# The last output projection of a two-layer decoder as Strassen's product of 7 for 8 (Winograd's form)

## The chip, the cores and the metric

One core of a Trainium2 chip. The time is device microseconds (us) of one execution. The engines are TensorE (PE: matrix products, and PEld, the loading of the stationary operand), VectorE (DVE), ScalarE (ACT), GpSimd (POOL) and SyncE (SP), whose queue issues nearly all transfers.

## The reference

Two layers on 1024 tokens of width 1024, in float32, each adding a normalized branch to its input, x <- x + RMSNorm_post(mixer(RMSNorm_pre(x))). Layer 0 is sliding-window attention. Layer 1 is a gated linear recurrence with 8 heads of 128:

```
proj = h @ w_in                      # q, f, i, z: 1024 columns each
o = chunked_gated_recurrence(silu(q), k(f), i, log_f(f))
o = o * rsqrt(mean(o * o) + eps) * gnorm_w        # per head
o = o.reshape(B, T, 1024) * silu(z)               # the gate
return o @ w_out                     # 1024 x 1024: the product that is changed
```

Call A the gated o (tokens x features) and B the matrix w_out (features x columns).

## The kernel before

**Precision.** Every matrix product of float32 operands is made of three TensorE products. Each operand is split in two parts of TensorE's float32 format: the high part is a rounded copy (ScalarE or GpSimd), the low part is what is left (VectorE). `product` (L219) issues high by high, high by low and low by high into the same PSUM bank.

**Weights.** All weight matrices lie in DRAM as blocks of 128x512 in the order of their use; 116 to 131 are w_out (first eight: columns 0 to 511, eight feature blocks; then columns 512 to 1023). `fetch` loads them on SP's queue into four raw buffers (`wraw`), `advance` splits them (`whi` on ScalarE L179, `wlo` on VectorE L180) into ten pairs of buffers, as soon as `used` has counted that the block which held the pair has served its last product. Before, each block of w_out serves eight units.

**Units.** `proj_nat(first, t)` (L243) computes 128 tokens (tile t) by 512 columns: eight feature blocks by three products, 24 instructions on TensorE into one bank. The activations are the stationary operand, in `act[k, half]` (feature block k, 512 tokens; `acth` and `actl`), the weights the moving one. PSUM has two banks for each of four tags (`mm`, `t`, `s`, `o`); a bank is written again only after it was emptied.

**Layer 1** (`mixer1`). First the value projections `i_unit(0, t)` of the first four heads (L876 empties them), beginning while the last rows of layer 0 are still normalized and transposed (L280, L204, L210); then, head by head, the query and gate projections `qf_unit` (L897 multiplies a query by its sigmoid, straight from the bank) with the recurrences `rec(h)` between them, which use the buffers `yn` and `S`; then the gate units `z_unit` (sigmoid on ScalarE, product on VectorE L1079, multiplication into `vo` on GpSimd L1080). `gated(half, ks)` transposes the gated o back on TensorE (L1071) and splits it from PSUM into `act` (L204, L210).

**The output projection** (`output1`): for both column halves c and eight token tiles t, one unit, then the sum of squares (ScalarE L1117), the product with the norm weight (VectorE L1118), and, when c is 1, the inverse root (GpSimd L258, L260), two VectorE instructions that scale a row and add x (L1131), and two stores. The last unit is cut in two halves of 256 columns. The second half of the last transposes comes behind the first unit.

**Order.** Each engine works through its own queue in the order in which a scheduler placed the program's instructions at build time; an instruction that waits holds up all behind it on that engine.

## Time and profile before

| what | us |
|---|---|
| three runs, median (lowest to highest) | 900.06 (899.93 to 900.25) |
| the profiled execution | 900.95 |
| its span | 899.1 |
| TensorE busy, share of the span | 878.8, 98% |
| VectorE busy | 556.3, 62% |
| ScalarE busy | 401.5, 45% |
| GpSimd busy | 326.1, 36% |

Times in the views are counted from the span's start. A row of a timeline gives start, length (of a run of like instructions, with their count), engine, line, operation, output and inputs, shapes, and in brackets how long the engine was idle before it and what released it. Matrix products overlap: the step from one start to the next is what one costs, not its length. A run's length with a count covers all of them. In the windows, columns are the engines' busy time in that stretch with the number of instructions, the granted TensorE clock, the share of the DMA engines, and GB/s.

### The profile page before, as it was taken

The numbers are of one execution on the slowest core, as the hardware profiler recorded it, in microseconds if no ns is written. First come the engines' busy times: TensorE is split into PE (matmuls) and PEld (weight loads), VectorE is DVE, ScalarE is ACT, GpSimd is POOL, SyncE is SP. The second block draws the span as 40 slices with busy tenths as digits, with TensorE's granted clock in tenths as the row PEclk, the third lists the DMA queues.
The fourth block names the chain that finished last, engine by engine and source line by source line (L and its number), as shares of the span: only waits on it lengthen the run. The fifth ranks groups of instructions, "written<-read, shape, count | busy, mean of one in ns | idle before, by whom it ended". The sixth has DMA issues, their size and how long they took to land.

```text
span 899.1 us, 14318 instructions
## 1 busy us (share of the span) xinstructions
PE 878.8 (98%) x5286; PEld 732.2 (81%) x5286; DVE 556.3 (62%) x900; ACT 401.5 (45%) x1048; POOL 326.1 (36%) x492
## 2 busy tenths in 40 slices
PE   6999999999999999999999999999999999999996
PEld 5887888888888888778888888888888788888885
DVE  7898887677898346852187873336877824262343
ACT  5635777767788233543223432333334224151211
POOL 4542644655676203320243532014434433220011
PEclk9999999999999999999999999999999999999998
DMA  9766455322132125422211010211111003041053
GB/s 339 266 201 184 136 169 142 92 71 82 48 92 82 47 95 175 154 106 72 70 48 36 17 43 1 83 49 34 37 36 48 1 1 94 1 135 53 24 187 121
DMA packets 55639, 82.61 MB, mean 92 GB/s; under 512 B 5128, under 2 KB 25224, under 8 KB 55560
## 3 DMA queue, kind: packets, MB, share of 16 engines
q1 hardware_dynamic: 55280, 81.54, 28.7%
q8 instruction: 43, 0.70, 0.3%
q14 instruction: 36, 0.29, 0.1%
q10 hardware_dynamic: 280, 0.07, 0.0%
HBM read 62.88 MB, written 16.88 MB: 89 GB/s over the span
## 4 chain that ended last, share of the span: by engine, by line
PE 78%; DVE 8%; issue 4%; DMA 4%; POOL 3%; ACT 1%; SPq 0%; DVEq 0%; POOLq 0%; ACTq 0%
PE psmm L222 48%; PE psmm L88 16%; PE pss L88 3%; PE pso L88 2%; DMA wraw<-in_w 2%; POOL rstd L260 2%; PE psk L1044 1%; PE pst L88 1%; PE pso L1057 1%; PE pso L1059 1%; POOL ms L258 1%; DMA xt<-in_xt 1%; PE pst L1038 1%; PE pst L1071 1%; DVE actl L88 1%
## 5 line engine op out<-in xcount | busy, mean ns | idle before, releaser
L222 PE MATMUL psmm<-whi,acth 128*128 128x512 f32 (+1 forms) x488 | 190.4, 391 | 1.1 <-DVE y L823 1.1
L222 PE MATMUL psmm<-whi,actl 128*128 128x512 f32 (+1 forms) x488 | 188.7, 388 | 0.0
L222 PE MATMUL psmm<-wlo,acth 128*128 128x512 f32 (+1 forms) x488 | 188.7, 387 | 0.0
L180 DVE TENSOR_TENSOR wlo<-wraw,whi 128x512 fp32r<-128x512 f32 x120 | 87.6, 740 | 94.1 <-ACT whi L179 88.6
L88 PE MATMUL psmm<-acth,whi 128*128 128x512 f32 x272 | 110.7, 407 | 1.7 <-ACT whi L88 1.7
L179 ACT ACTIVATE whi<-wraw 128x512 fp32r<-128x512 f32 x112 | 70.1, 630 | 87.9 <-PE psmm L222 66.9
L222 PEld LDWEIGHTS psmm<-whi,acth 128*128 128x128 f32 x488 | 91.7, 188 | 20.2 <-DVE y L823 1.8
L88 PE MATMUL psmm<-actl,whi 128*128 128x512 f32 x272 | 107.6, 396 | 0.2 <-DVE actl L88 0.2
L88 PE MATMUL psmm<-acth,wlo 128*128 128x512 f32 x272 | 107.7, 396 | 0.0
L222 PEld LDWEIGHTS psmm<-whi,actl 128*128 128x128 f32 x488 | 91.7, 188 | 18.4
L222 PEld LDWEIGHTS psmm<-wlo,acth 128*128 128x128 f32 x488 | 91.7, 188 | 17.9
L222 PE MATMUL psmm<-acth,whi 128*128 128x512 f32 x256 | 101.1, 395 | 0.2 <-DVE qf L897 0.2
L222 PE MATMUL psmm<-acth,wlo 128*128 128x512 f32 x256 | 100.4, 392 | 0.0
L222 PE MATMUL psmm<-actl,whi 128*128 128x512 f32 x256 | 100.2, 392 | 0.0
L708 ACT ACTIVATE sm<-sm,st 128x129 f32<-128x129 f32 x128 | 49.9, 392 | 26.6 <-DVE st L706 26.5
L88 PEld LDWEIGHTS psmm<-acth,wlo 128*128 128x128 f32 x272 | 51.7, 190 | 11.7 <-DVE wlo L88 0.2
L905 POOL TENSOR_SCALAR gate<-gate,lbt 128x512 f32<-128x512 f32 x16 | 17.8, 1111 | 118.9 <-ACT gate L903 108.4
L88 PEld LDWEIGHTS psmm<-acth,whi 128*128 128x128 f32 x272 | 52.0, 191 | 10.5 <-ACT whi L88 2.0
L88 PEld LDWEIGHTS psmm<-actl,whi 128*128 128x128 f32 x272 | 51.9, 191 | 8.7 <-DVE actl L88 0.7
L222 PEld LDWEIGHTS psmm<-acth,whi 128*128 128x128 f32 x256 | 48.1, 188 | 10.7 <-DVE qf L897 0.9
L222 PEld LDWEIGHTS psmm<-acth,wlo 128*128 128x128 f32 x256 | 48.1, 188 | 10.0
L222 PEld LDWEIGHTS psmm<-actl,whi 128*128 128x128 f32 x256 | 48.1, 188 | 9.5
(268 smaller groups left out, 1624.6 us busy)
## 6 DMA issues: line engine op xcount, KB each, us to landing
wraw<-in_w SPq DMA_DIRECT2D x132, 256.0 KB
QS<-qd SPq DMA_DIRECT2D x16, 512.0 KB
xr<-in_x SPq DMA_DIRECT2D x8, 512.0 KB
x1d<-xn SPq DMA_DIRECT2D x8, 512.0 KB
xr<-x1d SPq DMA_DIRECT2D x8, 512.0 KB
out_dram<-xn SPq DMA_DIRECT2D x16, 256.0 KB
o<-in_xt SPq DMA_DIRECT2D x8, 256.0 KB
xt<-in_x SPq DMA_DIRECT2D x4, 512.0 KB
```

What stands on the lines that cost most here:

```text
L88: return (lambda *a, **k: self.tc.keep_in_program_order(f(*a, **k))) if self.on else f
L179: nc.scalar.activation(hi, raw, AF.Copy)
L180: W["split_ins"][i] = v.tensor_tensor(lo, raw, hi.bitcast(F32), op=ALU.subtract)
L222: W["mm"] = pe.matmul(ps, a, b, start=(k == 0 and i == 0), stop=(k == NK - 1 and i == 2))
L258: keep(g.tensor_scalar(m, ms, eps, 1.0, op0=ALU.add, op1=ALU.mult))
L260: W["rstd"] = keep(g.tensor_tensor(r, m, nhalf[:, :width], op=ALU.pow))
L708: W["exp"] = nc.scalar.activation(sm[:, h, :], sm[:, h, :], AF.Exp, bias=nm[:, h:h + 1], scale=-1.0, accum_out=dn[:, h:h + 1])
L905: nc.gpsimd.tensor_scalar(dst, dst, ol, lb, op0=ALU.mult, op1=ALU.add)
L1038: nc.tensor.transpose(pt[:, i, :], Y[:, c * P:(c + 1) * P], ident)
L1044: nc.tensor.matmul(pk[:, i, :], yn[:, c, :], vt[:, c, hc], start=True, stop=True)
L1057: nc.tensor.matmul(po[:, i, :], sc[:, c, :], vt[:, c, hc], start=True, stop=(c == 0))
L1059: nc.tensor.matmul(po[:, i, :], X[:, c * P:(c + 1) * P], S[:, c, :], start=False, stop=True)
```

## The change

A and B are cut into 2 x 2 quarters (A11: tokens 0 to 511, features 0 to 511; A21: tokens 512 to 1023, the same features; B11: features 0 to 511, columns 0 to 511). In place of eight quarter products there are seven, M1 to M7, in this order:

| | activations | weights | then, for four token tiles each |
|---|---|---|---|
| M1 | A11 | B11 | copied to `p1`; the bank is kept |
| M2 | S3 = A11 - A21 | B22 - B12 (`td0`) | copied to `u3` |
| M3 | S2 = A22 - S3 | T2 = B22 - B12 + B11 (`td1`) | added to `p1`, that to `u3` |
| M4 | A22 | B21 - T2 (`td2`) | plus `u3`: second tokens, first columns |
| M5 | S1 = A21 + A22 | B12 - B11 (`td3`) | plus `u3`: second tokens, second columns, rows finished; the bank is kept |
| M6 | S4 = A12 - S2 | B22 | into the banks of M5; plus `p1`: first tokens, second columns |
| M7 | A12 | B21 | into the banks of M1: first tokens, first columns, rows finished |

A part of an M is 128 tokens by 512 columns by four feature blocks: 12 TensorE instructions, into a bank of its own (M1 in `mm` and `s`, the others in `t` and `o`). A weight block serves four parts.

The 16 sums of weights are made on VectorE in four groups among the first value projections (`weight_sums`): each loads four blocks into `yn` and `S`, makes four sums in place and stores them in DRAM (`td`), from where `fetch` reads them like any weight. The activations' sums, 16 instructions, are made on VectorE too, from unsplit transposed copies (`af`, in part laid over `vo`), and then split (`split`). The last row block is no longer cut in halves. The transposes stand between the last gate units, sixteen of them in M1. The second half of the gate units uses buffers of the last stage's pool, `fin1`.

Three places show what the change moves. First VectorE in the first value projections (`bq`: the sums' buffers; `wlo`: low halves of weights; L897, L906: the first query product). Before:

```order
L210 SCALAR_TENSOR_TENSOR actl7_1_135<-pst_4133,cst_72,acth7_1_134 128x512
L180 TENSOR_TENSOR wlo0_90<-wraw2_102,whi0_80 128x512
L180 TENSOR_TENSOR wlo1_91<-wraw3_103,whi1_81 128x512
L180 TENSOR_TENSOR wlo2_92<-wraw0_100,whi2_82 128x512
L180 TENSOR_TENSOR wlo3_93<-wraw1_101,whi3_83 128x512
L180 TENSOR_TENSOR wlo8_98<-wraw2_102,whi8_88 128x512
L180 TENSOR_TENSOR wlo9_99<-wraw3_103,whi9_89 128x512
L180 TENSOR_TENSOR wlo4_94<-wraw0_100,whi4_84 128x512
L180 TENSOR_TENSOR wlo5_95<-wraw1_101,whi5_85 128x512
L897 TENSOR_TENSOR qf_4412<-psmm_4387,sg_4413 128x512
```

And now, from the second group of sums on (the first stands right ahead of it):

```order
L1089 TENSOR_TENSOR bq_4251<-bq_4252,bq_4251 128x512
L1090 TENSOR_TENSOR bq_4251<-bq_4251 128x512
L188 TENSOR_TENSOR wlo0_94<-wraw2_106,whi0_84 128x512
L188 TENSOR_TENSOR wlo1_95<-wraw3_107,whi1_85 128x512
L188 TENSOR_TENSOR wlo2_96<-wraw0_104,whi2_86 128x512
L188 TENSOR_TENSOR wlo3_97<-wraw1_105,whi3_87 128x512
L1087 TENSOR_TENSOR bq_4318<-bq_4318 128x512
L188 TENSOR_TENSOR wlo8_102<-wraw2_106,whi8_92 128x512
L1088 TENSOR_TENSOR bq_4318<-bq_4318,bq_4317 128x512
L1089 TENSOR_TENSOR bq_4317<-bq_4318,bq_4317 128x512
L1090 TENSOR_TENSOR bq_4317<-bq_4317 128x512
L188 TENSOR_TENSOR wlo9_103<-wraw3_107,whi9_93 128x512
```

Two groups stand ahead of the weights' low halves, the third among them, ahead of the first query product; the fourth stands behind that product.

Second TensorE at the end of the last gate unit (`pst`: transposes of the gated o). Before:

```order
L222 MATMUL psmm_7573<-whi3_83,actl7_1_135 128x512
L1071 MATMUL pst_7626<-cst_72,o0_136 128x128 x4
L1071 MATMUL pst_7633<-cst_72,o0_136 128x128 x4
L1071 MATMUL pst_7640<-cst_72,o0_136 128x128 x4
L1071 MATMUL pst_7647<-cst_72,o0_136 128x128 x4
L222 MATMUL psmm_7663<-whi8_88,acth0_0_104 128x512
```

And now, behind 29 of M1's products (`psmm_7781` is one of its banks):

```order
L230 MATMUL psmm_7781<-wlo4_98,acth2_0_116 128x512
L230 MATMUL psmm_7781<-whi4_88,actl2_0_117 128x512
L230 MATMUL psmm_7781<-whi5_89,acth3_0_120 128x512
L1134 MATMUL pst_7769<-cst_76,vo1_3478 128x128
L1134 MATMUL pst_7775<-cst_76,vo1_3478 128x128
```

These need the last gate; before, sixteen transposes stood right behind it and sixteen behind the first output unit.

Third VectorE at the change from M3 to M4 (`p1`, `u3`: the sums; L1231: the first result of M4; `actl`, `wlo`: low halves):

```order
L188 TENSOR_TENSOR wlo1_95<-wraw1_105,whi1_85 128x512
L1127 TENSOR_TENSOR actl2_1_119<-af2_7383,acth2_1_118 128x512
L1221 TENSOR_TENSOR p1_0_7397<-psmm_7953,p1_0_7397 128x512
L1221 TENSOR_TENSOR p1_1_7398<-psmm_7971,p1_1_7398 128x512
L1127 TENSOR_TENSOR actl3_1_123<-af3_7384,acth3_1_122 128x512
L1221 TENSOR_TENSOR p1_2_7399<-psmm_7989,p1_2_7399 128x512
L1222 TENSOR_TENSOR u3_0_7401<-u3_0_7401,p1_0_7397 128x512
```

Before there was nothing of the kind: VectorE had the row's product L1118 once in a unit. The first L1221 is the 36th instruction from the first sum of S2 (L1208) on, and empties the bank that M4's first part writes.

The diff:

```diff
...
+        td = [dp.tile([4 * P, 512], F32, name=f"td{i}") for i in range(4)]
...
-        NS = I["w"].shape[0]
+        B1 = 116
+        SRC = [I["w"][i] for i in range(B1)]
+        quarter = lambda q: [I["w"][B1 + 4 * q + k] for k in range(4)]
+        sums_of = lambda i: [td[i][k * P:(k + 1) * P, :] for k in range(4)]
+        SRC += quarter(0) + sums_of(0) + sums_of(1) + sums_of(2) + sums_of(3) + quarter(3) + quarter(1)
+        NS = len(SRC)
...
         def fetch(end):
             while W["fetch"] < min(end, NS):
                 f = W["fetch"]
-                W["dmas"][f] = sy.dma_start(wraw[f % NR], I["w"][f])
+                W["dmas"][f] = sy.dma_start(wraw[f % NR], SRC[f])
...
-            W["left"][i] = W["left"].get(i, 8) - 1
+            W["left"][i] = W["left"].get(i, 8 if i < B1 else 4) - 1
...
-        def product(ps, k, stat, mov):
+        def product(ps, k, stat, mov, first=0, last=NK - 1):
-                W["mm"] = pe.matmul(ps, a, b, start=(k == 0 and i == 0), stop=(k == NK - 1 and i == 2))
+                W["mm"] = pe.matmul(ps, a, b, start=(k == first and i == 0), stop=(k == last and i == 2),
+                                    skip_group_check=first is None)
...
-            def gated(half, ks):
...
+            def weight_sums(k):
+                b = [rp.tile([P, 2, 512], F32, tag=t, name="bq") for t in ("yn", "S")]
+                b11, b21, b12, b22 = (x[:, i, :] for x in b for i in range(2))
+                for q, x in enumerate((b11, b21, b12, b22)):
+                    nc.sync.dma_start(x, I["w"][B1 + 4 * q + k])
+                v.tensor_tensor(b22, b22, b12, op=ALU.subtract)
+                v.tensor_tensor(b12, b12, b11, op=ALU.subtract)
+                v.tensor_tensor(b11, b22, b11, op=ALU.add)
+                v.tensor_tensor(b21, b21, b11, op=ALU.subtract)
+                for d, x in zip(td, (b22, b11, b21, b12)):
+                    nc.sync.dma_start(d[k * P:(k + 1) * P, :], x)
+            ws = [lambda k=k: weight_sums(k) for k in range(4)]
+            rc = lambda h: [lambda: rec(h)]
+            i0 = iu(0)
+            plan = i0[:1] + ws[:1] + i0[1:3] + ws[1:2] + i0[3:5] + ws[2:3] + i0[5:7] + ws[3:] + i0[7:]
+            plan += qf(0) + ([zeros] if fast else []) + qf(1) + rc(0) + qf(2) + rc(1) + qf(3) + rc(2) + iu(1) + rc(3)
+            plan += qf(4) + qf(5) + rc(4) + qf(6) + rc(5) + qf(7) + rc(6) + zu[:2] + rc(7) + zu[2:]
+            for u in plan:
+                u()
...
+        def final1(vo, fp):
+            wpost = fp.tile([P, D], F32, name="wpost1")
+            nc.sync.dma_start(wpost, I["bc"][2:3, :].to_broadcast([P, D]))
+            ssall = fp.tile([P, 2, 9], F32, name="ssall")
+            af = {(k, 0): fp.tile([P, 512], F32, name=f"af{k}") for k in range(NK)}
+            af.update({(k, 1): vo[k // 4][:, k % 4, :] for k in range(NK)})
+            late = [vo[k // 4][:, 4 + k % 4, :] for k in range(NK)]
+            s3 = late[:4]
+            s2p = [(fp.tile([P, 512], F32R, name=f"s2h{k}"), fp.tile([P, 512], F32R, name=f"s2l{k}")) for k in range(4)]
+            p1 = [fp.tile([P, 512], F32, name=f"p1_{t}") for t in range(4)]
+            u3 = [fp.tile([P, 512], F32, name=f"u3_{t}") for t in range(4)]
+            def split(pair, x):
+                nc.scalar.activation(pair[0], x, AF.Copy)
+                v.tensor_tensor(pair[1], x, pair[0].bitcast(F32), op=ALU.subtract)
+            def turned(half, ks):
                 for k in ks:
-                    pt = pp.tile([P, 512], F32, tag="tso"[k % 3], name="pst")
+                    pt = pp.tile([P, 512], F32, tag="to"[k % 2], name="pst")
                     for j in range(4):
                         nc.tensor.transpose(pt[:, j * P:(j + 1) * P],
                                             vo[k // 4][:, half * 4 + j, (k % 4) * P:(k % 4 + 1) * P], ident)
-                    act_from_psum(k, half, pt, cst[:, C_GN:C_GN + 1])
...
-        def output1(fp, last_half):
...
+                    nc.scalar.activation(af[k, half], pt, AF.Copy, scale=cst[:, C_GN:C_GN + 1])
+            def part(ps, left, e, t, more, done=True, cols=(0, 512)):
+                c = slice(t * P, (t + 1) * P)
+                for k in range(4):
+                    hi, lo = left[k]
+                    product(ps, k, (hi[:, c], lo[:, c]), weight(e, k, *cols), None if more else 0, 3)
+                    if done:
+                        used(e + k)
+            def row_part(c, t, y, x, cs, ss):
+                jk = fp.tile([P, 512], F32, tag="sg", bufs=2, name="jk")
+                nc.scalar.activation(jk[:, :cs.stop - cs.start], y, AF.Square, scale=D ** -0.5, accum_out=ss)
+                v.tensor_tensor(x, y, wpost[:, c * 512 + cs.start:c * 512 + cs.stop], op=ALU.mult)
+            def add_eps(ss, eps):
+                nc.gpsimd.tensor_scalar(ss, ss, eps, 1.0, op0=ALU.add, op1=ALU.mult)
+            xrs = {}
+            def x_rows(t):
+                xrs[t] = fp.tile([P, D], F32, tag="xr", bufs=5, name="xr")
+                nc.sync.dma_start(xrs[t], x1d[t * P:(t + 1) * P, :])
+            def finish(t, ss, eps, y0, y1):
                 r = rstd_of(fp, ss, 1, eps)
...
+                xr = xrs[t]
+                for i, yh in enumerate((y0, y1)):
                     cs = slice(i * 512, (i + 1) * 512)
...
+                    v.scalar_tensor_tensor(xr[:, cs], yh, r, xr[:, cs], op0=ALU.mult, op1=ALU.add)
+                    nc.sync.dma_start(out[t * P:(t + 1) * P, cs], xr[:, cs])
+            def z(c, *ts):
+                for t in ts:
+                    z_unit(fp, vo, c, t)
+            quad = lambda k0, half: [act[k0 + k, half] for k in range(4)]
+            E = [B1 + 4 * i for i in range(7)]
+            banks = ["mm", "mm", "s", "s"]
+            whole = slice(0, 512)
+            turned(0, (0, 1))
+            z(1, 0)
+            turned(0, (2, 3))
+            z(1, 1)
+            turned(1, (0, 1))
+            z(1, 2)
+            turned(1, (2, 3))
+            z(1, 3)
+            for k in range(4):
+                v.tensor_tensor(s3[k], af[k, 0], af[k, 1], op=ALU.subtract)
+                split(act[k, 0], af[k, 0])
+            z(1, 4)
+            turned(0, (4, 5))
+            z(1, 5)
+            turned(0, (6, 7))
+            z(1, 6)
+            for k in range(4, 8):
+                split(act[k, 0], af[k, 0])
+            z(1, 7)
+            p12 = []
+            for t in range(4):
+                p12.append(mm(tag=banks[t]))
+                part(p12[t], quad(0, 0), E[0], t, False)
+                nc.scalar.activation(p1[t], p12[t], AF.Copy)
+                split(act[t, 1], s3[t])
+                if t < 2:
+                    turned(1, (4 + 2 * t, 5 + 2 * t))
+            for k in range(4):
+                v.tensor_tensor(af[k, 0], af[4 + k, 1], s3[k], op=ALU.subtract)
+                split(s2p[k], af[k, 0])
+            for t in range(4):
+                ps = mm(tag="to"[t % 2])
+                part(ps, quad(0, 1), E[1], t, False)
+                nc.scalar.activation(u3[t], ps, AF.Copy)
+                split(act[4 + t, 1], af[4 + t, 1])
+                v.tensor_tensor(af[t, 1], af[t, 1], af[4 + t, 1], op=ALU.add)
+                split(act[t, 0], af[t, 1])
+            for t in range(4):
+                ps = mm(tag="to"[t % 2])
+                part(ps, s2p, E[2], t, False)
+                v.tensor_tensor(p1[t], ps, p1[t], op=ALU.add)
+                v.tensor_tensor(u3[t], u3[t], p1[t], op=ALU.add)
+                v.tensor_tensor(af[t, 0], af[4 + t, 0], af[t, 0], op=ALU.subtract)
+                split(act[t, 1], af[t, 0])
+            for t in range(4):
+                ps = mm(tag="to"[t % 2])
+                part(ps, quad(4, 1), E[3], t, False)
+                x_rows(4 + t)
+                v.tensor_tensor(s3[t], ps, u3[t], op=ALU.add)
+                ss = ssall[:, 0, 4 + t:5 + t]
+                row_part(0, 4 + t, s3[t], s3[t], whole, ss)
+                add_eps(ss, EPS)
+            p53 = []
+            for t in range(4):
+                p53.append(mm(tag="to"[t % 2]))
+                part(p53[t], quad(0, 0), E[4], t, False)
+                v.tensor_tensor(u3[t], p53[t], u3[t], op=ALU.add)
+                ss = ssall[:, 1, 4 + t:5 + t]
+                row_part(1, 4 + t, u3[t], u3[t], whole, ss)
+                finish(4 + t, ss, ssall[:, 0, 4 + t:5 + t], s3[t], u3[t])
+            for t in range(4):
+                part(p53[t], quad(0, 1), E[5], t, True)
+                x_rows(t)
+                v.tensor_tensor(p1[t], p53[t], p1[t], op=ALU.add)
+                ss = ssall[:, 1, t:t + 1]
+                row_part(1, t, p1[t], p1[t], whole, ss)
+                add_eps(ss, EPS)
+            for t in range(4):
+                part(p12[t], quad(4, 0), E[6], t, True)
+                ss = ssall[:, 0, t:t + 1]
+                y = late[4 + t]
+                row_part(0, t, p12[t], y, whole, ss)
+                finish(t, ss, ssall[:, 1, t:t + 1], y, p1[t])
         def network(fast):
             keep, oc = layer0()
...
                     output0(oc, fp)
                 with pool("rec", "left") as rp:
-                    last_half = mixer1(fast, vo, rp)
+                    mixer1(fast, vo, rp)
                 with pool("fin1", "left") as fp:
-                    output1(fp, last_half)
+                    final1(vo, fp)
```

More of the change, by code (lines that the diff above doesn't have):

```diff
@@ L1065, in rec @@
                     v.tensor_tensor(vt[:, b4 * 4:b4 * 4 + 4, hc], po, r.unsqueeze(2).to_broadcast([P, 4, P]), op=ALU.mult)
-            def gated(half, ks):
+            QF = [(0, 0), (1, 0), (0, 1), (1, 1)]
+            qf = lambda h: [lambda u=u: qf_unit(h, *u) for u in QF]
+            iu = lambda c: [lambda t=t: i_unit(c, t) for t in range(8)]
+            zu = [lambda t=t: z_unit(rp, vo, 0, t) for t in range(8)]
+            def weight_sums(k):
[9 more added lines that the diff above has]
+                    nc.sync.dma_start(d[k * P:(k + 1) * P, :], x)
@@ new lines, in z_unit @@
+        def z_unit(pool, vo, c, t):
+            ps = proj_nat(100 + 8 * c, t)
+            sg = pool.tile([P, 512], F32, tag="sg", bufs=2, name="sg")
+            nc.scalar.activation(sg, ps, AF.Sigmoid)
+            v.tensor_tensor(sg, ps, sg, op=ALU.mult)
+            nc.gpsimd.tensor_tensor(vo[c][:, t, :], vo[c][:, t, :], sg, op=ALU.mult)
+        def final1(vo, fp):
[13 more added lines that the diff above has]
+            def turned(half, ks):
@@ L1082, in mixer1 @@
-            QF = [(0, 0), (1, 0), (0, 1), (1, 1)]
-            qf = lambda h: [lambda u=u: qf_unit(h, *u) for u in QF]
-            iu = lambda c: [lambda t=t: i_unit(c, t) for t in range(8)]
-            zu = lambda c: [lambda t=t: z_unit(c, t) for t in range(8)]
-            rc = lambda h: [lambda: rec(h)]
-            plan = iu(0) + qf(0) + ([zeros] if fast else []) + qf(1) + rc(0) + qf(2) + rc(1) + qf(3) + rc(2) + iu(1) + rc(3)
-            plan += qf(4) + qf(5) + rc(4) + qf(6) + rc(5) + qf(7) + rc(6) + zu(0)[:2] + rc(7) + zu(0)[2:]
```

49 lines of the change are left out of this document (removed).

## The prediction

> **What bounds the kernel now.** I read the page's busy times first, then the chain of waits over the last 140 us, then windows of the same stretch.
>
> ```profile
> PE 878.8 (98%) x5286; PEld 732.2 (81%) x5286; DVE 556.3 (62%) x900; ACT 401.5 (45%) x1048; POOL 326.1 (36%) x492
> ```
>
> TensorE (PE) has no idle time to speak of; every other engine has. The chain (start, length, what) says the same of the stage that is changed:
>
> ```profile
> 788.73 10.91 PE psmm L222 x48
> 799.64 1.75 PE pst L1071 x16
> 801.39 5.46 PE psmm L222 x24
> 806.85 1.75 PE pst L1071 x16
> 808.59 81.94 PE psmm L222 x384
> ...
> 892.79 0.75 DVE xn L1131
> ```
>
> The last two gate units end at 799.64. After 16 transposes, the output projection is 5.46 + 81.94 = 87.4 us of products, with no wait between them, up to 890.53. What remains, to the end of the span at 899.1, is the tail of the last row block. So a product that disappears here is paid out in full, as long as nothing else becomes late. The other engines have room there:
>
> ```profile
> 820.00:840.00 20.00, 20.00 (x90) 16.56 (x89) 2.77 (x4) 2.34 (x8) 0.77 (x4) 1.00 0.00 1
> ```
>
> In these 20 us the columns after PE and weight loads are VectorE 2.77, ScalarE 2.34 and GpSimd 0.77 us busy; the granted clock is 1.00.
>
> **Products removed.** The 48 products of the first chain row take 10.91 / 48 = 0.2273 us each. The last unit is cut into two halves:
>
> ```profile
> 884.38 0.39 PE L222 MATMUL psmm<-whi,actl 128*128 128x512 f32 x1
> 884.61 0.28 PE L222 MATMUL psmm<-whi,acth 128*128 128x256 f32 x1
> ...
> 890.24 0.28 PE L222 MATMUL psmm<-whi,actl 128*128 128x256 f32 x1
> ```
>
> From 884.61 to 890.24 there are 47 steps, 0.1198 us each, so its 48 half products cost 5.75 us. The other 14 units of the 81.94 us cost (81.94 - 5.75) / 336 = 0.2268 us a product. The new stage has 7 x 4 x 4 x 3 = 336 products of full width: 76.2 us. **Saved: 87.4 - 76.2 = 11.2 us.** The number of transposes stays at 64. They stand among products now, which is free by an earlier stage of this kernel:
>
> ```profile
> 400.04 0.39 PE L222 MATMUL psmm<-wlo,acth 128*128 128x512 f32 x1
> 400.27 0.60 PE L280 MATMUL pst<-cst,hn 128*128 128x128 f32 x4
> 400.62 0.48 PE L222 MATMUL psmm<-whi,actl 128*128 128x512 f32 x1
> 400.94 0.40 PE L222 MATMUL psmm<-whi,acth 128*128 128x512 f32 x1
> ```
>
> Four transposes and a product take 400.94 - 400.27 = 0.67 us, no more than 4 x 0.109 (1.75 / 16) + 0.227. The Trainium skill ("TensorE: Matmul & The Clock Gate", Back-to-back issue gap) gives about 131 ns for a 512-wide matmul in a sustained stream; by it 48 full products would save some 6.3 us, called an estimate, but this trace shows 0.227 us, and the row decides.
>
> **The tail.** The last row block is no longer halved, so its end is that of the block before it:
>
> ```profile
> 886.58 1.42 DVE L1131 SCALAR_TENSOR_TENSOR xn<-y,rstd,xr 128x512 f32<-128x512 f32 x2 [0.30 <-POOL rstd L260]
> ...
> 892.12 1.42 DVE L1131 SCALAR_TENSOR_TENSOR xn<-y,rstd,xr 128x512 f32<-128x512 f32 x2 [0.64 <-POOL rstd L260]
> ```
>
> A full block's last product slot ends at 884.61 and its row at 888.00: 3.39 us. The halved block's ends at 890.36 and 893.54: 3.18 us. The change loses **0.2 us**. The 5.56 us after 893.54 (store and end) stay, since the last two stores have the same size.
>
> **Does VectorE keep up?** This is the term that I can only bound. From the last gate unit on, the built order has 102 VectorE instructions of 128x512 and 66 on ScalarE. With 48 transposes done before it, that gate unit ends at 799.64 + 1.75 = 801.4. Then, without stalls, M1 (with its 16 transposes) ends at 814.0, M2 at 824.9, M3 at 835.8, M4 at 846.7, M5 at 857.5, M6 at 868.4 and M7 at 879.3. Prices:
>
> ```profile
> 787.71 0.69 DVE L1079 TENSOR_TENSOR sg<-psmm,sg 128x512 f32<-128x512 f32 x1 [3.79 <-ACT sg L1078]
> 788.32 2.72 DVE L210 SCALAR_TENSOR_TENSOR actl<-pst,cst,acth 128x512 fp32r<-128x512 f32 x4
> 794.92 0.69 DVE L1079 TENSOR_TENSOR sg<-psmm,sg 128x512 f32<-128x512 f32 x1 [3.88 <-ACT sg L1078]
> 795.57 3.59 DVE L180 TENSOR_TENSOR wlo<-wraw,whi 128x512 fp32r<-128x512 f32 x4
> ```
>
> ```profile
> 794.90 2.72 ACT L179 ACTIVATE whi<-wraw 128x512 fp32r<-128x512 f32 x4
> ```
>
> ```profile
> 795.75 1.66 POOL L1080 TENSOR_TENSOR vo<-vo,sg 128x512 f32<-128x512 f32 x1 [5.90 <-DVE sg L1079]
> ```
>
> Queued behind one another, VectorE instructions start 0.61 us apart (787.71 to 788.32) and last 0.69; beside a GpSimd multiply they take 3.59 / 4 = 0.90. I take 0.61 to 0.69: after the last gate multiply GpSimd has only 128x1 instructions. ScalarE takes 2.72 / 4 = 0.68.
>
> VectorE's run of sums starts when the first late transposes are evicted. Those wait for the last gate unit's sigmoid, product and GpSimd multiply, and by the order stand 29 products and 12 transposes into M1: 6.6 + 1.3 us, then their own and 0.7 for the eviction, so about 810.3. Two things downstream are due. The low half of S2's last block (s2l3, the 25th instruction) is read 25 products into M3, at 830.6; it is there at 825.6 to 827.6. The eviction of M3's first bank (the sum into p1, L1221 of the new kernel, the 36th) must precede M4, which reuses the bank at 835.8; it is done at 832.3 to 835.1. From there VectorE gains: 62 instructions remain, 38 to 43 us, for 43.5 us of M4 to M7. ScalarE: the last s2h is its 22nd instruction from there, 810.3 + 22 x 0.68 = 825.3, in time. So **0 us**, with 0.7 us in hand at the slower price; at 0.90 it would be late (below). A weight block now serves 2.7 us of products, not 5.4; its two splits cost 0.68 and 0.69 on their engines, and ten slots hold it ahead.
>
> **The weight sums.** 16 VectorE instructions (11 us at 0.69), 16 loads and 16 stores of 256 KB on SP's queue. Here VectorE was idle and SP had nothing to fetch:
>
> ```profile
> 402.76 0.75 DVE L210 SCALAR_TENSOR_TENSOR actl<-pst,cst,acth 128x512 fp32r<-128x512 f32 x1 [0.39 <-ACT acth L204]
> 418.62 2.74 DVE L180 TENSOR_TENSOR wlo<-wraw,whi 128x512 fp32r<-128x512 f32 x4 [15.11 <-ACT whi L179]
> ...
> 428.79 0.69 DVE L897 TENSOR_TENSOR qf<-psmm,sg 128x512 f32<-128x512 f32 x1 [2.54 <-ACT sg L896]
> ```
>
> ```profile
> 388.95 0.42 SPq L879 DMA_DIRECT2D m<-in_msk  x1
> 419.35 48.38 SPq L143 DMA_DIRECT2D wraw<-in_w  x16
> ```
>
> ```profile
> 422.03 0.63 ACT L179 ACTIVATE whi<-wraw 128x512 fp32r<-128x512 f32 x1 [1.39 <-DMA wraw<-in_w]
> 423.29 0.63 ACT L179 ACTIVATE whi<-wraw 128x512 fp32r<-128x512 f32 x1 [0.63 <-DMA wraw<-in_w]
> ```
>
> A block issued at 419.35 is read at 422.03 (2.7 us), the next 1.3 us later. A round is four loads (2.7 + 3 x 1.3 = 6.6), four sums (2.8) and four stores (by the same price 6.6): 16 us one after the other, some 10 as ordered, since sums begin with the first pair of loads and the next loads with the first landed stores. The first sums wait for the norm's last split (403.5) and last till 406; the second round's last till about 416.5, before the weight splits at 418.6; the third's loads land by 424.3, and its sums, with weight splits between them, push the first query product (L897, L906 in the new kernel) from 428.79 to about 429.5. It empties one of two banks:
>
> ```profile
> 428.16 0.60 ACT L896 ACTIVATE sg<-psmm 128x512 f32<-128x512 f32 x1 [1.36 <-PE psmm L222]
> ```
>
> Its unit ends at 428.16, the next one 10.91 / 2 = 5.45 us later, at 433.6, and the one after that writes the bank again. Done at 430.2, the product has 3.4 us in hand: **0 us**. What is queued behind a late load is this product on VectorE; behind a late store it is the next weight fetches on SP, whose blocks the second head's units read only from 428.16 - 5.45 + 4 x 5.45 = 444.5 on. Without that cover the 11 us would be paid whole. SP also gets the row of norm weights and five loads of x rows, 512 KB each, ahead of the last fetches for M2: 12 x 1.3 = 16 us, issued once the seventh recurrence's buffers are free, some 40 us before M2. GpSimd's small additions only change places.
>
> **Sum.** 11.2 - 0.2 = 11.0 us. The profiled execution took 900.95 us at a span of 899.1, the runs 900.06 in the median, 0.9 less. The span becomes 888.1; the time of the runs **889.1 us**.
>
> **Rivals.** B, VectorE a little late: its waits on ScalarE within each pair of a split count into the pace. At 0.78 us the 36th instruction ends at 810.3 + 28.1 = 838.4, so M4 waits 2.6 us for p1's eviction; the 98 instructions from 810.3 on end at 886.7, 4.0 us after the forecast's last row (M7's 879.3 + 3.4 = 882.7): 893 us. For it: the margin of 0.7 us. Against it: the pace of 0.61 to 0.69 in the rows.
>
> C, **slower**: VectorE becomes the bound. At 0.90 us its 98 instructions from 810.3 end at 898.5, against 893.54 now: 905 us. It decides from (893.54 - 810.3) / 98 = 0.85 us on; below that the change wins. For it: the 0.90 of the row beside a GpSimd multiply. Against it: 0.77 us of GpSimd in 20 us in the window above. The Trainium skill ("SBUF — State Buffer", Who interferes with whom) has a VectorE instruction with two SBUF inputs contend with a GpSimd instruction that reads SBUF; the 0.90 agrees, and by that rule the splits and sums are the kind that is hit, but only while GpSimd works on large tiles.
>
> D, the sums' transfers come late: if each of three rounds takes 3 us more, the query product is done at 439.2, not 430.2, 5.6 us past its due time: 894.7 us. For it: loads that wait for stores, stores that wait for VectorE, all in one queue. Against it: the queue was empty from 389.4 to 419.35.
>
> E, the stage doesn't get shorter: products in groups of 12 instead of 24, two banks held to the end, cost what the fewer products save: 900. Against it: 0.227 us holds across unit borders in the chain.
>
> **Chances.** No stall 0.64, B 0.15, C 0.08, D 0.09, E 0.04. A difference of 0.2% (1.8 us) is what a measurement of this kernel can tell from none. Faster: no stall, B and D, 0.88. Same: E, 0.04. Slower: C, 0.08. The range goes from 888.3 (the 0.2 us of the tail, and as much of pace, the other way) to 895.0 (B and D in their middle), which leaves C, E and the ends of B out.
>
> **What would show it.** Right: TensorE instructions fall by 72 (408 to 336 in this stage); the chain's last stretch is one run of products up to 879.3 with no "issue" or VectorE piece; VectorE in it averages 0.7 us or less; the sums stand at 403 to 441 and TensorE's windows there stay full; last row at 882.7. Wrong: waits of TensorE for L1221 (B), a VectorE busy throughout to the end (C), waits of psmm for qf near 435 (D), a product step other than 0.227 us (E).

## The result, and the profile after

| what | before | after |
|---|---|---|
| median (lowest to highest) of 4 runs each, us | 899.99 (899.28 to 900.25) | 888.46 (888.05 to 888.91) |
| ratio, 95% interval | | 0.9873 (0.9856 to 0.989) |
| the profiled execution, us | 900.95 | 888.05 |
| its span, us | 899.1 | 886.3 |

The forecast was 889.1 us, with a range of 888.3 to 895.0. The kernel became 11.5 us faster by the medians; 11.0 were forecast. The busy times on the page of the changed kernel:

```profile
PE 867.1 (98%) x5214; PEld 721.1 (81%) x5214; DVE 604.0 (68%) x975; ACT 426.9 (48%) x1094; POOL 333.0 (38%) x491
```

TensorE has 72 instructions fewer (5286 before), as foretold, and is still busy for 98% of the span. VectorE has 75 instructions more and is busy 47.7 us longer, which the time does not show. The chain of waits of the changed kernel (start, length, what) is TensorE's own up to the first of the last four row blocks:

```profile
789.13 10.90 PE psmm L230 x48
800.03 0.22 PE pst L1134 x2
800.25 2.30 PE psmm L230 x10
802.55 0.11 PE pst L1134
802.66 0.46 PE psmm L230 x2
803.12 0.98 PE pst L1134 x9
804.11 3.88 PE psmm L230 x17
807.99 0.22 PE pst L1134 x2
808.21 0.46 PE psmm L230 x2
808.67 0.22 PE pst L1134 x2
808.89 61.37 PE psmm L230 x269
...
880.88 0.74 DVE xr L1167
```

After the last gate unit (to 800.03 in the chain, which counts a piece to the end of its last product's shown length), 16 transposes stand among the first products. From 808.89 on there is one run of products. The chain leaves TensorE at 870.26 only because it follows the finishing of a row from there; TensorE goes on. Windows of the changed kernel over the same stretch show that (columns: PE, weight loads, VectorE, ScalarE, GpSimd busy, granted clock, share of the DMA engines, GB/s):

```profile
813.00:824.00 11.00, 11.00 (x50) 9.08 (x50) 11.00 (x20) 11.00 (x23) 0.00 (x0) 1.00 0.28 76
824.00:835.00 11.00, 11.00 (x49) 8.84 (x48) 10.71 (x19) 4.60 (x9) 0.00 (x0) 1.00 0.39 116
835.00:846.00 11.00, 11.00 (x50) 9.13 (x49) 8.10 (x14) 4.24 (x10) 1.58 (x3) 1.00 0.31 96
868.00:878.00 10.00, 10.00 (x45) 8.27 (x45) 6.73 (x11) 2.79 (x8) 3.19 (x8) 1.00 0.40 154
```

Where VectorE had 2.77 us of work in 20 us before, it now has 21.7 in 22, and in the first of these windows ScalarE is full too. TensorE is at 11.00 of 11.00 in each. Its last two products, by the timeline, and the piece after them:

```profile
877.79 0.39 PE L230 MATMUL psmm<-wlo,acth 128*128 128x512 f32 x1
878.02 0.39 PE L230 MATMUL psmm<-whi,actl 128*128 128x512 f32 x1
```

With the last slot of 0.23 us the products end at 878.25, and the last row at 880.88 + 0.74 = 881.62.

**Where the 12.8 us between the two spans come from.** Three parts can be told apart. The first is everything ahead of the first changed instruction, whose mark is the last split of the norm of layer 1: VectorE at 402.76 in the profile before, and here

```profile
401.55 0.75 DVE L218 SCALAR_TENSOR_TENSOR actl<-pst,cst,acth 128x512 fp32r<-128x512 f32 x1 [0.38 <-ACT acth L212]
```

That is 1.2 us earlier, with the same work. The second part goes from this mark to the end of the last row: 490.78 us before (402.76 to 893.54), 480.07 now (401.55 to 881.62): 10.7 us less. The third is what follows the last row: 5.56 before, 4.68 now. The change cannot act on the first part. Whether the third is the change's is a question for a second profile, below.

### The profile page after: what moved, and what is told of

It reads as the page before. It is cut to its first block, busy times and chain, and to the rows that moved or that the text cites. A ratio compares the mean times of both kernels' runs of the same rounds, so it can differ in the third digit from the quotient of the medians.

```text
span 886.3 us, 14409 instructions
## 1 busy us (share of the span) xinstructions
PE 867.1 (98%) x5214; PEld 721.1 (81%) x5214; DVE 604.0 (68%) x975; ACT 426.9 (48%) x1094; POOL 333.0 (38%) x491
## 4 chain that ended last, share of the span: by engine, by line
PE 81%; DVE 7%; issue 4%; POOL 3%; ACT 2%; DMA 2%; DVEq 0%; POOLq 0%; ACTq 0%
PE psmm L230 47%; PE psmm L88 20%; PE pss L88 3%; PE pso L88 2%; POOL rstd L269 2%; PE psk L1053 1%; PE pst L88 1%; PE pso L1066 1%; PE pso L1068 1%; POOL ms L267 1%; PE pst L1047 1%; PE pst L1134 1%; PE psd L1004 1%; DMA qd<-qh 1%; DMA out_dram<-xr 1%
## 5 line engine op out<-in xcount | busy, mean ns | idle before, releaser
L230 PE MATMUL psmm<-whi,acth 128*128 128x512 f32 x448 | 176.3, 395 | 1.1 <-DVE y L832 1.1
L230 PE MATMUL psmm<-wlo,acth 128*128 128x512 f32 x448 | 175.0, 391 | 0.0
L230 PE MATMUL psmm<-whi,actl 128*128 128x512 f32 x448 | 174.9, 392 | 0.0
L188 DVE TENSOR_TENSOR wlo<-wraw,whi 128x512 fp32r<-128x512 f32 x132 | 96.3, 742 | 71.2 <-ACT whi L187 67.5
L187 ACT ACTIVATE whi<-wraw 128x512 fp32r<-128x512 f32 x124 | 77.5, 631 | 94.9 <-PE psmm L230 72.6
L230 PEld LDWEIGHTS psmm<-whi,acth 128*128 128x128 f32 x448 | 84.1, 188 | 19.1 <-DVE y L832 1.9
L230 PEld LDWEIGHTS psmm<-whi,actl 128*128 128x128 f32 x448 | 84.1, 188 | 17.2
L230 PEld LDWEIGHTS psmm<-wlo,acth 128*128 128x128 f32 x448 | 84.2, 188 | 16.7
L230 PEld LDWEIGHTS psmm<-acth,whi 128*128 128x128 f32 x256 | 48.1, 188 | 10.8 <-DVE qf L906 0.9
```

What stands on the lines that cost most here:

```text
L187: nc.scalar.activation(hi, raw, AF.Copy)
L188: W["split_ins"][i] = v.tensor_tensor(lo, raw, hi.bitcast(F32), op=ALU.subtract)
L230: W["mm"] = pe.matmul(ps, a, b, start=(k == first and i == 0), stop=(k == last and i == 2), skip_group_check=first is None)
```

## The experiments

Each profile was taken apart in the same three parts. The middle one, called the changed part from here on, turned out to repeat within 0.1 us, ten times better than the run's time, so verdicts on less than 1 us go by it.

### The same two kernels again

> The changed kernel once more, in more rounds. If the gain is the 48 products (11 us less TensorE time, nothing else moved), the ratio stays within 0.9873 +- 0.0015, and the changed part of the profile (from the last split of the norm of layer 1, 402.76 us before and 401.55 us after, to the last row) is again 10.5 to 11 us shorter, while the 1.2 us at the start and the 0.9 us after the last row may fall out differently. If those two belong to the change, they come back with the same size.

> A second profile of the kernel before. The profiled runs differ by 1.2 us ahead of the first changed instruction and by 0.9 us after the last row (5.56 us before, 4.68 after). If these belong to the run and not to the change, a second profile has the last split of the norm nearer to the changed kernel's 401.6 to 402.2 and less than 5.56 us after the last row; if they belong to the kernel, they come back: 402.8 and 5.5 us. The part between stays at 490.8 us either way.

The changed kernel took 888.82 us (888.67 to 889.6), ratio 0.9876 (0.986 to 0.9893). Its marks are 402.22 and 882.38: a changed part of 480.16 us, and 4.82 us after it. The kernel before, in its second profile, by the timeline of VectorE:

```profile
402.21 0.75 DVE L210 SCALAR_TENSOR_TENSOR actl<-pst,cst,acth 128x512 fp32r<-128x512 f32 x1 [0.38 <-ACT acth L204]
...
891.61 1.42 DVE L1131 SCALAR_TENSOR_TENSOR xn<-y,rstd,xr 128x512 f32<-128x512 f32 x2 [0.63 <-POOL rstd L260]
```

The mark is at 402.21, where the changed kernel had it in its second profile: the first 1.2 us belong to the run. The changed part is 490.82 us, as in the first profile. After the last row (893.03) come 5.37 us to the span's end of 898.4. So the third part does belong to the kernel: 5.56 and 5.37 before; 4.68 and 4.82 after, and between 4.64 and 4.91 in all variants of the changed kernel. The SP queue shows one difference there. Its last store in the first profile before, and in the first one after:

```profile
893.57 1.22 SPq L1132 DMA_DIRECT2D out_dram<-xn  x1
```

```profile
881.65 0.33 SPq L1168 DMA_DIRECT2D out_dram<-xr  x1
```

To issue a store of the same size took 1.22 us in the one (0.99 in its second profile) and 0.33 in the other (0.42). From the end of that issue to the end of the span it is 4.3 to 4.4 us in all four profiles (899.1 - 894.79 before, 886.3 - 881.98 after), so the difference lies in the issue itself; why it is longer was not tried.

### The eighth product put back

```diff
             for t in range(4):
+                ps = mm(tag="to"[t % 2])
+                part(ps, quad(4, 1), E[6], t, False, done=False)
+            for t in range(4):
                 part(p12[t], quad(4, 0), E[6], t, True)
```

> Puts the eighth quarter product back as work alone: 48 more TensorE products of full width (A22 by B21, four parts into banks that are not kept) between M6 and M7; the result doesn't use them, nothing else changes. Theory that the gain is the product count: 48 times 0.228 = 10.9 us slower than the changed kernel, 899.4, so within 1 us of the kernel before. Rival, the stage was bounded by VectorE, or by groups of 12 with kept banks (rivals C and E of the forecast): the added products fall in part into waiting time, and it costs 0 to 6 us, 888.5 to 894.5.

Measured: 899.63 us (899.18 to 900.32), ratio to the kernel before 0.9994 (0.9985 to 1.0004). The chain's long run of products, 61.37 us for 269 in the changed kernel, is now

```profile
809.06 72.25 PE psmm L230 x317
```

48 products and 10.88 us more. The changed part is 490.90 us, against 480.1 without them: 10.8 us, 0.225 us a product. The gain is the product count. Rival C falls, since beside a VectorE that is the bound 48 products could not cost their full price; rival E, a stage that does not get shorter, falls with the time of the changed kernel itself, and with all 384 products in groups of 12 the stage takes what it took in groups of 24 (changed part 490.90 against 490.82). This is also the cleanest answer on the price by which the forecast chose between a row (0.227) and the Trainium skill's 131 ns ("TensorE: Matmul & The Clock Gate", Back-to-back issue gap): the row holds, and 48 products at 131 ns would have been 6.3 us.

### The sums of weights

Left out, stored twice, stored four times. The edits:

```diff
-        SRC += quarter(0) + sums_of(0) + sums_of(1) + sums_of(2) + sums_of(3) + quarter(3) + quarter(1)
+        SRC += quarter(0) + quarter(2) + quarter(3) + quarter(1) + quarter(2) + quarter(3) + quarter(1)
...
-            plan = i0[:1] + ws[:1] + i0[1:3] + ws[1:2] + i0[3:5] + ws[2:3] + i0[5:7] + ws[3:] + i0[7:]
+            plan = list(i0)
```

```diff
-                for d, x in zip(td, (b22, b11, b21, b12)):
+                for d, d2, x in zip(td, tx, (b22, b11, b21, b12)):
                     nc.sync.dma_start(d[k * P:(k + 1) * P, :], x)
+                    nc.sync.dma_start(d2[k * P:(k + 1) * P, :], x)
```

(`tx` are further tiles in DRAM; the third kernel stores into three of them for each sum).

> Leaves out the 16 sums of weights with their 16 stores (the products M2 to M5 read plain quarters of w_out instead, so the output is another). Theory that the sums lie wholly beside TensorE's work: the same time as the changed kernel, 888.5 within 0.5 us. Rival, the sums cost something at their place (late query product, or SP's queue): 1 to 5 us faster, 883 to 887.5; the first query product was then late enough to hold up a unit, which would show as a wait of the products for that product's bank before 445 us.

> Each sum of weights is stored twice (16 more stores of 256 KB on SP's queue), the rest is as it was. It asks how much room the forecast's transfers had. By the forecast's price (a transfer each 1.3 us) a round of four loads and four stores gets 5.2 us longer, the third group's sums are done 10 us later (about 438 instead of 428 us) and, being ahead of the first query product on VectorE, make it 4 to 6 us late for its bank: about 893 us. Rival: the next group's loads wait only for the first landed store of a buffer, and the queue takes a transfer faster than 1.3 us; then the query product is 0 to 3 us later, within its 3.4 us, and the time is that of the changed kernel, 888.5.

> Each sum of weights is stored four times (48 stores more than the changed kernel has). With two stores the time did not move, since a transfer took 0.7 us and not 1.3, and since the third group of sums then stood behind the first query product. Theory that what is left of rival D is SP's queue, whose next weight fetches stand behind the stores: 64 stores at 0.7 us are 45 us from 403 on, so that the weights which the second head's units read from 444 on come up to 8 us late; with fetches standing between the groups, I expect 0 to 5 us: 889 to 894. If TensorE still waits for nothing there, the transfers have more room than four times what they use.

Without the sums: 888.92 us (888.42 to 889.0), changed part 480.10 us. They cost nothing. Their place in the changed kernel, by VectorE's timeline:

```profile
410.59 0.69 DVE L1087 TENSOR_TENSOR bq<-bq 128x512 f32<-128x512 f32 x1 [5.51 <-DMA bq<-in_w]
...
428.38 0.69 DVE L906 TENSOR_TENSOR qf<-psmm,sg 128x512 f32<-128x512 f32 x1 [1.17 <-ACT sg L905]
```

The first query product (L906) starts 26.8 us after the mark (428.38 - 401.55); before it was 26.0 (428.79 - 402.76). So it is 0.8 us later, where the forecast had 0.7, with 3.4 in hand.

Stored twice: 888.66 us (887.73 to 889.52), changed part 480.00. The query product is 1.6 us later than in the changed kernel by its mark (430.57 against 402.10):

```profile
430.57 0.69 DVE L907 TENSOR_TENSOR qf<-psmm,sg 128x512 f32<-128x512 f32 x1 [1.22 <-ACT sg L906]
```

This does not quite ask what it was meant to ask: with the longer transfers the scheduler put the third group of sums behind this product, not ahead of it.

Stored four times: 893.08 us in one run, changed part 484.69, so 4.6 us longer. Here TensorE does wait, for a later query product. VectorE's timeline, and then TensorE's:

```profile
471.64 0.69 DVE L1089 TENSOR_TENSOR bq<-bq 128x512 f32<-128x512 f32 x1 [1.10 <-DMA bq<-in_w]
472.25 2.28 DVE L974 TENSOR_TENSOR_SCAN U<-gate,F 128x1024 f32<-128x1024 f32 x1
...
479.68 0.68 DVE L1091 TENSOR_TENSOR bq<-bq 128x512 f32<-128x512 f32 x1
480.39 0.69 DVE L907 TENSOR_TENSOR qf<-psmm,sg 128x512 f32<-128x512 f32 x1
```

```profile
481.13 0.50 PE L231 MATMUL psmm<-acth,whi 128*128 128x512 f32 x1 [2.89 <-DVE qf L907]
```

The last group of sums has slid among the scans of a recurrence; one of its loads is late by 1.1 us, the scans queue behind it, and the query product behind them. That is rival D's mechanism (a query product queued behind a late load), but at a later product, near 480 us and not 435, and only at four times the stores; that the time lies within 2 us of D's 894.7 does not confirm its price. The expectation had put it on the weight fetches; no product waited for a weight there.

### How much room VectorE has

Six, then twelve, more VectorE instructions ahead of S2's splits; and in a third kernel, GpSimd products beside them.

```diff
                 v.tensor_tensor(af[k, 0], af[4 + k, 1], s3[k], op=ALU.subtract)
+                for _ in range(3):
+                    v.tensor_tensor(af[k, 0], af[k, 0], af[k, 0], op=ALU.max)
                 split(s2p[k], af[k, 0])
```

(twelve; for six, 2, 2, 1 and 1 of them).

> Six more VectorE instructions of 128x512 (a maximum of a block with itself, which leaves it as it is) among the sums for S2, ahead of everything that M3 and M4 wait for: 6 x 0.60 = 3.6 us more on VectorE there. The profile of the changed kernel puts the first eviction into p1 4.1 us ahead of its due time and the low half of S2's last block 5.5 us ahead. Theory that this is all the room there is, and that it is room: no change, 888.7 within 0.5. Rival, by the forecast's own number (0.7 us in hand): 2.9 us slower, 891.6.

> Twelve of the same instructions: 7.2 us more on VectorE. Theory (room of 4.1 us at the bank that M4 writes, 5.5 us at S2's last block): M4 starts 7.2 - 4.1 = 3.1 us late, all in all 891 to 892 us, with TensorE waiting for the sum into p1. By the forecast's 0.7 us: 6.5 us slower, 895.2. Rival, the order leaves VectorE much more room than this since its queue is rearranged around the wait: 888.7.

First the changed kernel's own rows for the two due places, S2's last block and the first eviction into p1:

```profile
823.32 0.68 DVE L1127 TENSOR_TENSOR s2l<-af,s2h 128x512 fp32r<-128x512 f32 x1
...
829.94 1.28 DVE L1221 TENSOR_TENSOR p<-psmm,p 128x512 f32<-128x512 f32 x2
```

The eviction is done at 829.94 + 0.68 = 830.6. M4's first product starts at 834.72, right behind M3's last one, so 4.1 us were in hand. Six more instructions: 888.53 us (887.81 to 889.05), changed part 480.12, and the eviction stands at

```profile
834.00 1.28 DVE L1223 TENSOR_TENSOR p<-psmm,p 128x512 f32<-128x512 f32 x2
```

done at 834.7, with M4 at 835.17: 0.5 us left, which is 4.1 - 3.6. The room is real and is used up, at no cost.

Twelve: 893.92 us (893.52 to 894.3), 2 us more than expected; the changed part is 485.46, 5.3 us longer. Two things differ from what I had written down. The wait is not at p1 but at S2's blocks, which the scheduler had put behind more of VectorE's work; by the list of waits TensorE waited 1.2 us for S2's high half and 1.9 for a low one. And 3.1 us of waits cost 5.3. TensorE's timeline shows what the rest is:

```profile
825.72 0.50 PE L230 MATMUL psmm<-whi,s2h 128*128 128x512 f32 x1 [1.24 <-ACT s2h L1126]
...
829.71 0.50 PE L230 MATMUL psmm<-whi,s2l 128*128 128x512 f32 x1 [1.86 <-DVE s2l L1127]
...
831.06 0.63 PE L230 MATMUL psmm<-wlo,s2h 128*128 128x512 f32 x1
...
834.04 0.52 PE L230 MATMUL psmm<-whi,s2l 128*128 128x512 f32 x1
```

After the second wait, seven products step at (834.04 - 831.06) / 7 = 0.426 us in place of 0.234: 1.3 us. Windows of the same place give the reason:

```profile
828.00:830.00 2.00, 0.29 (x1) 0.29 (x2) 2.00 (x4) 0.90 (x2) 0.00 (x0) 1.00 0.26 80
830.00:832.00 2.00, 2.00 (x8) 1.52 (x8) 2.00 (x5) 0.64 (x1) 0.00 (x0) 0.72 0.58 198
832.00:834.00 2.00, 2.00 (x6) 1.56 (x5) 2.00 (x5) 1.32 (x3) 0.00 (x0) 0.50 0.81 247
834.00:836.00 2.00, 2.00 (x9) 1.64 (x8) 2.00 (x4) 1.37 (x3) 0.00 (x0) 0.92 0.00 0
```

The granted clock falls to 0.50 behind the waits and is back after some 3.4 us (in the three windows that it touches, 0.28 x 2 / 0.5 + 2 + 0.08 x 2 / 0.5). By the steps, the two waits cost 1.39 and 2.01 us (step less 0.23), the slow products 1.34, and five more products at the ends of waits and clock changes some 0.1 each: 5.3 in all. In the kernel with four stores the clock falls to 0.50 as well, behind its one wait of 2.89 us (part 4.6 us longer). By the Trainium skill ("TensorE: Matmul & The Clock Gate", What's actually happening) the clock is halved after an idle window of about 3.4 us and whole again after about 3.4 us of sustained work; the half and the length of the slow stretch agree with the runs here, but it takes less to get there: an idle stretch of 2.9 us, or of 1.2 and 1.9 with eight products between them, was enough.

```diff
-            def split(pair, x):
+            def split(pair, x, beside=False):
...
+                if beside:
+                    nz[0] += 1
+                    nc.gpsimd.tensor_tensor(late[4 + nz[0] % 4], af[4 + nz[0] % 4, 0], af[4 + nz[0] % 4, 0], op=ALU.mult)
...
-                split(s2p[k], af[k, 0])
+                split(s2p[k], af[k, 0], True)
...
```

(and the same `True` at the three other splits for M2 to M4; `nz` counts them).

> Adds 16 GpSimd products of 128x512 (1.66 us each, 27 us), one beside each of the 16 splits of the activations for M2 to M4; they read plain copies and write a buffer that is dead, so that VectorE waits for none of them. Theory that rival C of the forecast was right in its mechanism and only lacked GpSimd work to set it off: a VectorE split beside them takes about 0.90 us instead of 0.60, the 36th instruction from 808.9 on ends near 808.9 + 36 x 0.90 = 841.3, M4 starts some 6 us late (834.7 now), and the last row with it, because VectorE's later run has only the ordinary slack: 893 to 896 us. Rival, the 0.90 had another cause: splits stay at 0.60 apart and the time is the changed kernel's, 888.7. By the Trainium skill (SBUF — State Buffer, Who interferes with whom) the first would hold, since the splits read two SBUF operands.

Measured: 895.92 us (895.67 to 896.4), ratio 0.9951 (0.9934 to 0.9968); changed part 487.09, 7.0 us longer. The timelines of VectorE and of GpSimd:

```profile
810.09 1.47 DVE L1213 TENSOR_TENSOR af<-vo,o 128x512 f32<-128x512 f32 x1 [1.98 <-ACT vo L1141]
811.48 1.52 DVE L1221 TENSOR_TENSOR o<-o,vo 128x512 f32<-128x512 f32 x1
...
827.40 1.52 DVE L1127 TENSOR_TENSOR actl<-vo,acth 128x512 fp32r<-128x512 f32 x1
828.84 0.68 DVE L188 TENSOR_TENSOR wlo<-wraw,whi 128x512 fp32r<-128x512 f32 x1
```

```profile
806.07 22.31 POOL L1130 TENSOR_TENSOR vo<-af 128x512 f32<-128x512 f32 x16
```

The 16 products ran in one stretch, not each beside its split. As long as they do, VectorE's instructions start 1.44 us apart ((827.40 - 810.09) / 12); from 828.84 on, with GpSimd idle, 0.60 again. So the mechanism of rival C is there, at a higher price than its 0.90 us: that row had been four VectorE instructions beside a single GpSimd product, so part of it was undisturbed. The expected time came out by an overestimate of how many instructions are hit and an underestimate of each: 13 times 0.84 is 10.9 us, against 36 times 0.30, 10.8. By the list of waits TensorE waited 3.9 us for low halves of S2 (0.75 and 3.13, three products between them) and 0.6 for p1. These 4.5 us of waits cost 7.0, for the granted clock was 0.50 from 830 to 832 us here too. By the Trainium skill ("SBUF — State Buffer", Who interferes with whom) VectorE instructions with two SBUF inputs contend with a GpSimd instruction that reads SBUF; the run agrees.

### Why the products saved less than forecast: M3

Count the stage from the slot end of the last gate product (its start plus 0.23 us) to the slot end of the last product. Before, the last gate product is

```profile
799.24 0.40 PE L222 MATMUL psmm<-whi,actl 128*128 128x512 f32 x1
```

so the stage goes from 799.47 to 890.36: 90.89 us with 32 transposes, where the forecast's terms give 87.4 + 2 x 1.75 = 90.9. In the changed kernel the last gate product and the first of M2 are

```profile
799.64 0.39 PE L230 MATMUL psmm<-whi,actl 128*128 128x512 f32 x1
...
812.60 0.39 PE L230 MATMUL psmm<-whi,acth 128*128 128x512 f32 x1
```

so the stage goes from 799.87 to 878.25: 78.38 us with 16 transposes, where the forecast's terms give 76.2 + 1.75 = 77.95. It is 0.43 us longer. M1 with its 16 transposes takes 12.73 us (812.60 - 799.87), 0.1 more than 48 x 0.2268 + 1.75 = 12.64; the rest is in M3. Windows from M3's first product to M4's first, and from there to M5's:

```profile
823.48:834.72 11.24, 11.24 (x50) 9.04 (x48) 10.95 (x19) 4.91 (x9) 0.00 (x0) 1.00 0.40 118
834.72:845.60 10.88, 10.88 (x49) 9.01 (x48) 7.98 (x13) 4.05 (x11) 1.35 (x3) 1.00 0.32 97
```

Both are full of products, 48 each (the counts take in a neighbour), and M3 is 0.36 us longer: 0.2342 us a product, not 0.2267. Three kernels ask why.

```diff
-                part(ps, s2p, E[2], t, False)
+                part(ps, quad(4, 0), E[2], t, False)
...
-                part(p12[t], quad(4, 0), E[6], t, True)
+                part(p12[t], s2p, E[6], t, True)
```

> Exchanges the activations of two products: M3 reads A22 from the ordinary buffers, M7 reads S2 from its own (the output is another, the amount of work the same). In the changed kernel M3 takes 11.24 us for its 48 products (0.2342 each) where M4 to M7 take 10.88 (0.2267); this is 0.36 of the 0.45 us that the products saved less than forecast. If S2's buffers are the reason, M3 falls to 10.88 and M7 rises to 11.2. If it is M3's place in time (both other engines full, weights that were stored only in this kernel) or the order of its products, M3 stays at 11.2 and M7 at 10.9. The whole time is the changed kernel's either way, 888.7.

The time was 887.86 us in one run. Windows of M3, and of M7 up to one step after its last product's start:

```profile
823.31:834.19 10.88, 10.88 (x49) 9.01 (x48) 10.88 (x19) 4.89 (x9) 0.00 (x0) 1.00 0.35 122
866.83:878.07 11.24, 11.24 (x49) 8.85 (x47) 7.69 (x12) 2.79 (x8) 3.81 (x8) 1.00 0.38 138
```

The slower step went with S2's buffers to M7. It is neither M3's place in time nor its weights. Then the buffers were laid elsewhere, with the same work:

```diff
             wpost = fp.tile([P, D], F32, name="wpost1")
+            s2p = [...]
             ssall = fp.tile([P, 2, 9], F32, name="ssall")
             af = ...
-            s2p = [...]
```

> S2's eight buffers are laid out ahead of the other buffers of the last stage, not behind `af`; nothing else changes, so their addresses are others. If the slower M3 comes from where these buffers lie, it changes from 11.24 us towards 10.88; if from anything else, it stays. The whole time within 0.4 us of the changed kernel's 888.7.

887.89 us in one run, changed part 479.68. M3:

```profile
823.53:834.41 10.88, 10.88 (x49) 9.01 (x48) 10.86 (x19) 4.89 (x9) 0.00 (x0) 1.00 0.37 122
```

By the built program's addresses, `ssall`, 72 bytes in each partition, stands ahead of them in the changed kernel, and every large buffer behind it begins 32 bytes past a multiple of 64; all other stationary operands of M1 to M7 begin on one. The last kernel moves `ssall` alone:

```diff
-            ssall = fp.tile([P, 2, 9], F32, name="ssall")
             af = ...
             s2p = ...
             u3 = ...
+            ssall = fp.tile([P, 2, 9], F32, name="ssall")
```

> The small buffer `ssall` (72 bytes a partition) is laid out behind the large buffers of the last stage instead of ahead of them. In the changed kernel everything behind it begins 32 bytes off a multiple of 64; now S2's buffers lie 96 bytes lower than there, on a multiple of 64, while the order of all buffers but `ssall` stays. If the slower M3 (11.24 us) is the alignment of the stationary operand, it takes 10.88 us, as it did with S2's buffers moved elsewhere. If it was the area in which they lay, it stays at 11.2. The whole time by alignment 0.36 us less than the changed kernel, 888.3 (not to be told apart in the times, only in the profile).

```profile
823.81:834.69 10.88, 10.88 (x49) 9.01 (x48) 10.86 (x19) 4.89 (x9) 0.00 (x0) 1.00 0.41 122
```

S2's buffers are 96 bytes from where they were, on a multiple of 64, and M3 takes 10.88 us. So the alignment makes the difference, not the area. Only these two offsets, 0 and 32 bytes, were tried, and why it costs time is open. The changed part is 479.72, 0.4 us shorter. Its time is 887.93 us (887.75 to 888.19), ratio 0.9863 (0.9847 to 0.988). It beats the kernel before and, by the changed part, the changed kernel too; beside the latter's 888.46 and 888.82 the times alone would hardly show it.

## Why the prediction was right, point by point

**Products removed (11.2 us).** The mechanism was right, and is shown by the eighth product put back. The term was 0.44 too large: the stage went from 90.89 to 78.38 us with 16 transposes fewer in it, so the products saved 90.89 - 78.38 - 1.75 = 10.76. The price before was right. The step that failed is that all products after the change cost the same 0.2268: M3's, with their stationary operand 32 bytes off, cost 0.2342, 0.36 us in all. The remaining 0.1 is M1's.

**Transposes among products (0).** Right within 0.1 us, by which M1 with its 16 transposes is longer than the sum of the prices; whether the transposes or the products beside them cost it is not shown.

**The tail (0.2 us lost).** The last row ends 881.62 - 878.25 = 3.37 us after its last product slot; 3.39 was forecast, 3.18 before.

**What follows the last row (5.56, "stays").** Wrong by 0.7 us, in favour of the change: 4.6 to 4.9 in all twelve profiles of the changed kernel and its variants, 5.4 and 5.6 before. The forecast reasoned from the stores' size; the difference lies in how long the issue of the last one takes, and its cause is open.

**VectorE keeps up (0).** Right, with more room than forecast: 4.1 us where it had 0.7 at the slower of its two paces (3.5 at the faster). The failed step is that slower pace: 0.69 us is how long an instruction lasts, but queued ones start before the one ahead has ended. From S2's first sum (808.86) on, 36 instructions at 0.60 give 830.5; the eviction ended at 830.6. Rival B thus had no pace to stand on; a late VectorE does hold TensorE up somewhere between 3.6 us (six added instructions, no cost) and 7.2 us (twelve), at S2's blocks rather than at p1. Rival C needs GpSimd work, of which there is none; with 16 products of it VectorE slows as C says, and the kernel is 7 us slower, though still not slower than before.

**The weight sums (0).** Right: leaving them out changes nothing, and the query product is 0.8 us later (0.7 forecast).

**The sum.** 10.76 - 0.19 for the tail gives 10.57; the changed part shrank by 10.7, so that 0.14 us lies elsewhere between the mark and the last gate unit. With 0.7 after the last row the kernel gains 11.4 us, and the medians say 11.5 (11.3 for the repeated runs). The forecast's 11.0 was near partly by luck: 0.44 too much in one term, 0.7 left out in another.

## What to carry to other kernels

Where TensorE is never idle, removing products pays their full start-to-start step, and everything else is a question of due times: for each place where it could wait, count the queued instructions ahead by their start-to-start step (0.60 us here), not by their length. Where each works on a buffer that the one just ahead has used, as in the first group of weight sums, the step is 0.72 (402.93, 403.66, 404.38 in the changed kernel). Such room ends abruptly: a wait of 2.9 us, or two of 1.2 and 1.9 close together, also halves the granted clock for some 3.4 us, so that 3.1 us of waits cost 5.3. Lay small odd-sized buffers behind the large ones: 72 bytes ahead of a stationary operand cost each product that reads it 3%.

## What the runs showed of the hardware that was not expected

- A product whose stationary operand begins 32 bytes past a multiple of 64 steps at 0.2342 us; on a multiple of 64, at 0.2267. A group of weight loads in M3 and one in 836 to 846 us, nearly all M4, of the changed kernel (count, busy us, mean ns, idle us) show that the load itself is no longer, 188 ns in both:

```profile
L230 PEld LDWEIGHTS psmm<-whi,s2l 128*128 128x128 f32 x16 | 3.0, 188 | 0.7
```

```profile
L230 PEld LDWEIGHTS psmm<-whi,actl 128*128 128x128 f32 x15 | 2.8, 188 | 0.6
```

- A VectorE instruction with two SBUF inputs beside an uninterrupted run of GpSimd products takes 1.44 us from start to start, against 0.60 alone.
- The granted clock falls to 0.50 after an idle stretch of 2.9 us, after two of 1.2 and 1.9 with eight products between, and after two of 0.75 and 3.1 with three between.
- Full VectorE and ScalarE (11.00 of 11.00 us each from 813 to 824, nearly all of M2) did not slow TensorE's step beside them: M2's 48 products took 823.48 - 812.60 = 10.88 us, 0.2267 each, the price of the kernel before.
